# Spreading row sums and norm factors over the partitions by small DMAs through DRAM instead of TensorE transposes

## The chip, the cores and the metric

The kernel runs on one core of one Trainium2 chip. The metric is the device time of one execution in microseconds (us). An interval worked out from such times is given where two kernels are compared.

## The reference

Two layers (DEPTH = 2) of an encoder with 512 tokens and 1024 channels. One projection of the layer's input feeds everything: a latent attention (branch A), a differential attention (branch B), their SiLU gates, and the merge gates. Then the two branches are merged, projected, and normalized.

```python
for l in range(DEPTH):
    h = x @ w_in[l]
    c_q, c_kv, k_r, gate_a, q_d, k_d, v_d, gate_b, gates = _split_cols(h)
    q_a = (_rms_norm(c_q, g_q[l]) @ w_q_up[l])           # 8 heads, rotary on 32 of 96
    kv = (_rms_norm(c_kv, g_kv[l]) @ w_kv_up[l])          # 8 heads, keys 64 and values 64
    o_a = _dense_attention(q_a, k_a, v_a, mla_scale)      # softmax over 512 keys
    y_a = (o_a * jax.nn.silu(gate_a)) @ w_branch_a[l]
    o_b = _differential_attention(q_b, k_b, v_b, lam, diff_scale)   # 4 heads, 2 softmax maps each
    o_b = _rms_norm(o_b, g_diff[l], eps=1e-5) * (1.0 - lam_init)
    y_b = (o_b * jax.nn.silu(gate_b)) @ w_branch_b[l]
    g = jax.nn.sigmoid(gates + b_merge[l])
    out = (g[..., :D_MODEL] * y_a + g[..., D_MODEL:] * y_b) @ w_out[l]
    x = _layer_norm(DEEPNORM_ALPHA * x + out, ln_gamma[l], ln_beta[l])
```

## The kernel before

Activations stand feature-major: 128 features on the partitions, all 512 tokens along the free dimension. Every fp32 operand is split into a leading part and an exact rest, and a product is three matmuls: `mm3` (L122 to L125). ScalarE (ACT) makes the leading part, VectorE (DVE) the rest: for weights these are L109 and L112 in `slot`, for other tiles L159 and L160 in `split`.

A projection of 128 columns of `w_in` (`proj`) is 24 matmuls of 128x512 into one of three PSUM banks called `acc`. Scores go to two banks `sc`, transposes to two banks `tr` (in traces `pstr`), and attention outputs to one bank `pv`.

**Latent attention (the MLA stage).** For each of 8 heads, `mla_scores` makes four tiles of scores (128 queries by 512 keys), and `soft` takes the row maximum on DVE (L169) and the exponential on ACT (L171), whose accumulator leaves the row sum: one number per query, queries on the partitions. `mla_values` transposes the exponentials chunk by chunk on TensorE (`keyT`, L178), splits them (ACT L180, DVE L181), and multiplies by the values into `pv` (L365, L366). Two heads make one output chunk `o` of 128 features by 512 tokens. Its row sums stand with the tokens on the partitions, but have to multiply along the free dimension. So after the odd head the kernel takes reciprocals (L375), writes each 64 times side by side (`rx`, L377, DVE), transposes the result by four TensorE transposes with the identity into a `tr` bank (L381), multiplies the gate chunk by it (L383), and then the output by the gate (L384).

**Differential attention.** For each of 4 heads, `diff_scores` and `diff_values` do the same with two maps. The RMS norm factor of a token (four columns of 128) is computed by DVE (L481, L482) and by a power on GpSimd (POOL, L484). `bcast` spreads it over the partitions with four transposes of a column that is read 128 times (L140). L487 multiplies the gate by it, L488 the output by the gate, and `split` makes the operand of the second branch projection.

**Order.** Each engine works through its own list in order. A scheduling layer fixes these lists when the kernel is built, from the order in which the code emits the operations, and it lets operations that it expects to be ready go ahead of others. The code emits the work in the order of `weave` and of the tables `fill` and `dfill`: `fill[h]` names the projections emitted behind MLA head h ("a2" is the gate chunk 2, "q0" and "k0" are the queries and keys of differential head 0). Temporary tiles of 128x512 have the tag `tmp` with three buffers; gate chunks have the tag `g` with two. All DMAs are issued by SyncE (SP): the weights come as 512 KB tiles (L103). GpSimd issues none.

Of the kernel before, what the change touches and what calls it, by code (L numbers as in the profile page):

```python
# [11 lines left out]
F32 = mybir.dt.float32  # L12
F32R = mybir.dt.float32r
AF = mybir.ActivationFunctionType
ALU = mybir.AluOpType
# [4 lines left out]
SEQ = 512  # L20
P = 128
# [10 lines left out]
# columns of w_in  # L32
# [3 lines left out]
# Weight slots of one layer, in order of use: each is [128, 1024].  # L36
# [9 lines left out]
# columns of the parameter table  # L46
# [4 lines left out]
def hybrid_trunk(ctx: ExitStack, tc: tile.TileContext, x, xT, wlat, wts, prm, dlam, gb, tab, rtab, out):  # L51
# [29 lines left out]
    # ---- constants  # L81
# [5 lines left out]
    # the clock of TensorE rises while the first loads are on their way  # L87
# [12 lines left out]
    # ---- weight slots: H is the leading part of w, L the exact rest  # L100
# [14 lines left out]
    # x, feature-major  # L115
# [11 lines left out]
    def proj(l, name):  # L127
        """128 columns of w_in, feature-major: [128 features, 512 tokens]."""
        hi, lo = slot(l, name)
        acc = pt_("acc")  # L130
        for k in range(KC):
            mm3(acc, hi[:, k * P:(k + 1) * P], lo[:, k * P:(k + 1) * P],
                xH[:, k, :], xL[:, k, :], k == 0, k == KC - 1)
        return acc

    def bcast(col):
        """columns [128 tokens, 4] -> [128, 512] with the token's value in every row."""
        b = pt_("tr")
        for t in range(NT):
            nc.tensor.transpose(b[:, t * P:(t + 1) * P], col[:, t:t + 1].broadcast_to([P, P]), ident)  # L140
        return b

    def silu2(acc):
        """2*silu of a gate chunk."""
        th = t2("tmp")
        nc.scalar.activation(th, acc, AF.Tanh, scale=0.5)
        g = t2("g")
        nc.vector.scalar_tensor_tensor(g, th, 1.0, acc, ALU.add, ALU.mult)
        return g
# [16 lines left out]
    def soft(S, sums):  # L166
        """exp(S - max) with its row sums."""
# [6 lines left out]
    def keyT(pts, c):  # L174
        """chunk c of the keys of p, transposed: [128 keys, 512 queries], split."""
# [8 lines left out]
    def layer(l, last):  # L184
# [3 lines left out]
        # ---- latents and the shared rotary key, token-major, with the RMS norms  # L188
# [65 lines left out]
        # ---- lambda  # L254
# [15 lines left out]
        # ---- key tiles of the even and the odd heads: 64 rows without, 2 x 32 rows with rotary  # L270
# [71 lines left out]
        def mla_scores(h, q):  # L342
# [4 lines left out]
            sums = opair[-1][1].rearrange("p (t e) -> p t e", e=2)  # L347
            pts = []
            for t in range(NT):
# [4 lines left out]
                yield pts  # L354

        def mla_values(h, pts):
# [16 lines left out]
            if e == 1:  # L373
                r = small(8)
                nc.vector.reciprocal(r, sums)  # L375
                rx = t2("tmp")
                nc.vector.tensor_scalar(rx.rearrange("p (a b) -> p a b", a=8),  # L377
                                        r.unsqueeze(2).broadcast_to([P, 8, 64]), 0.5, None, ALU.mult)
                b = pt_("tr")
                for t in range(NT):  # L380
                    nc.tensor.transpose(b[:, t * P:(t + 1) * P], rx[:, t * P:(t + 1) * P], ident)  # L381
                g = gate_acc.pop(c)
                nc.vector.tensor_tensor(g, g, b, ALU.mult)  # L383
                nc.vector.tensor_tensor(o, o, g, ALU.mult)  # L384
                yA.append(split(o, "y"))
            yield

        # ---- differential attention
# [33 lines left out]
        def diff_v(c):  # L422
            """the values of heads 2c and 2c+1: [128 tokens, 2 x 128] for each token tile"""
# [68 lines left out]
        # ---- branch projections under their merge gates  # L492
# [28 lines left out]
        # ---- emission  # L521
        def weave(*gens):
            """One step of each in turn; what the first yields."""
# [33 lines left out]
        fill = {0: ["q0"], 1: ["k0"], 2: [], 3: ["q1"], 4: ["k1", "a2"], 5: [], 6: ["a3"], 7: []}  # L557
# [45 lines left out]
        # ---- out projection, residual, layer norm  # L603
# [79 lines left out]
# ---- host side: layout only  # L683
# [98 lines left out]
```

## Time and profile before

| | |
|---|---|
| median of 3 runs | 864.25 us (863.44 to 864.85) |
| profiled execution, first to last instruction | 862.9 us |
| TensorE (PE) matmuls busy | 848.3 us, 98% |
| VectorE busy | 588.8 us, 68% |
| ScalarE busy | 429.6 us, 50% |
| GpSimd busy | 21.8 us, 3% |
| mean DMA rate | 88 GB/s |

The one profiled execution's own time is known as this span; it lies 1.35 us under the median of the runs. "Busy" for PE counts from a matmul's start to its modelled end, and matmuls overlap, so the distance from start to start is the better measure of what one costs. The stages of layer 0 are, by the first and last instructions of their lines, about 45 to 160 us (MLA), 190 to 345 us (differential attention and branch projections woven with it), and after that the merge gates and the output projection; layer 1 repeats them from about 470 us.

### The profile page before, as it was taken

The page shows a single profiled execution, that of the slowest core. Times are in us where ns is not written, and L with a number is a line of the kernel's source. Part 1 is how long each engine was busy: PE and PEld are TensorE (multiplying, and loading weights), DVE is VectorE, ACT ScalarE, POOL GpSimd, SP SyncE. Part 2 cuts the span into 40 slices and gives each one's busy share as a digit, 9 for nine tenths or more (in the row PEclk, how much of TensorE's full clock was granted, in tenths as well). Part 3 has the DMA queues.
Part 4 walks back from the last instruction along what each step waited for, and adds up shares of the span by engine and source line. Part 5 has one row for each costly group of instructions (what it writes and reads, how often), then busy time and mean ns, then how long its engine had stood idle before and what let it go on. Part 6 is the DMA issues. An engine that isn't in the chain of part 4 may idle for free.

```text
span 862.9 us, 11026 instructions
## 1 busy us (share of the span) xinstructions
PE 848.3 (98%) x4121; PEld 693.9 (80%) x4121; DVE 588.8 (68%) x1066; ACT 429.6 (50%) x843; POOL 21.8 (3%) x30
## 2 busy tenths in 40 slices
PE   9899999999999999999999999999999999999996
PEld 7678777878888878888897778788788888788885
DVE  6689998686646745455857899876667466545457
ACT  5767776463534633332236776755546354433310
POOL 0100000000000000000110000000000000000001
PEclk9999999999999999999999999999999999999998
DMA  8310111213222352233514010112222234422322
GB/s 299 116 43 31 38 56 55 74 32 99 90 74 74 122 177 78 95 97 117 182 41 143 13 36 26 49 49 74 74 74 74 79 92 123 151 97 95 98 74 97
DMA packets 27701, 75.70 MB, mean 88 GB/s; under 512 B 3200, under 2 KB 7808, under 8 KB 27648
## 3 DMA queue, kind: packets, MB, share of 16 engines
q1 hardware_dynamic: 27648, 75.01, 27.0%
q8 instruction: 32, 0.52, 0.3%
q14 instruction: 21, 0.17, 0.1%
HBM read 70.80 MB, written 4.19 MB: 87 GB/s over the span
## 4 chain that ended last, share of the span: by engine, by line
PE 89%; ACT 5%; DVE 3%; DMA 1%; issue 1%; POOL 0%; SPq 0%; DVEq 0%; ACTq 0%
PE psacc L124 22%; PE psacc L123 22%; PE psacc L125 22%; PE pstr L178 4%; PE pspv L365 2%; PE pspv L123 2%; PE pssc L123 2%; PE pspv L366 2%; PE pssc L124 2%; PE pssc L125 2%; PE pspv L124 1%; PE pspv L125 1%; ACT wh L109 1%; PE pssc L444 1%; DMA wr<-in_wts_dram 1%; PE pssc L449 1%
## 5 line engine op out<-in xcount | busy, mean ns | idle before, releaser
L112 DVE TENSOR_TENSOR wl<-wr,wh 128x512 fp32r<-128x512 f32 x192 | 126.9, 686 | 152.3 <-ACT wh L109 152.0
L123 PE MATMUL psacc<-xH,wh 128*128 128x512 f32 x512 | 203.5, 398 | 0.0
L125 PE MATMUL psacc<-xH,wl 128*128 128x512 f32 x512 | 203.4, 397 | 0.0
L124 PE MATMUL psacc<-xL,wh 128*128 128x512 f32 x512 | 203.2, 397 | 0.0
L109 ACT CAST wh<-wr 128x1024 fp32r<-128x1024 f32 x96 | 100.6, 1048 | 180.6 <-PE psacc L124 95.6
L123 PEld LDWEIGHTS psacc<-xH,wh 128*128 128x128 f32 x512 | 96.2, 188 | 21.9
L124 PEld LDWEIGHTS psacc<-xL,wh 128*128 128x128 f32 x512 | 96.2, 188 | 21.8
L125 PEld LDWEIGHTS psacc<-xH,wl 128*128 128x128 f32 x512 | 96.3, 188 | 21.3
L171 ACT ACTIVATE p<-pssc,sm 128x512 f32<-128x512 f32 x128 | 88.2, 690 | 25.1 <-DVE sm L169 24.4
L169 DVE TENSOR_REDUCE sm<-pssc 128x1 f32<-128x512 f32 x128 | 86.7, 683 | 4.5 <-PE pssc L125 1.8
L181 DVE TENSOR_TENSOR pt<-pstr,pt 128x512 fp32r<-128x512 f32 x96 | 64.9, 685 | 8.5 <-ACT pt L180 7.9
L180 ACT CAST pt<-pstr 128x512 fp32r<-128x512 f32 x96 | 55.6, 586 | 27.8 <-PE pstr L178 25.7
L178 PE MATMUL pstr<-ident,p 128*128 128x128 f32 x384 | 57.3, 272 | 0.0
L178 PEld LDWEIGHTS pstr<-ident,p 128*128 128x128 f32 x384 | 47.4, 141 | 12.0 <-ACT p L171 0.5
L123 PE MATMUL psacc<-wh,xH 128*128 128x256 f32 (+1 forms) x164 | 49.1, 299 | 0.1
L124 PE MATMUL psacc<-wl,xH 128*128 128x256 f32 (+1 forms) x164 | 48.7, 297 | 0.2 <-DVE wl L202 0.2
L125 PE MATMUL psacc<-wh,xL 128*128 128x256 f32 (+1 forms) x164 | 48.3, 295 | 0.0
L123 PEld LDWEIGHTS psacc<-wh,xH 128*128 128x128 f32 x164 | 30.9, 188 | 1.5 <-ACT xH L119 0.6
L124 PEld LDWEIGHTS psacc<-wl,xH 128*128 128x128 f32 x164 | 30.9, 188 | 0.8 <-DVE wl L202 0.4
L125 PEld LDWEIGHTS psacc<-wh,xL 128*128 128x128 f32 x164 | 30.8, 188 | 0.2
L365 PE MATMUL pspv<-pt,vs 128*128 128x512 f32 x64 | 29.1, 455 | 0.3
L123 PE MATMUL pssc<-kv,qm 128*128 128x512 f32 x64 | 26.7, 422 | 0.4 <-ACT kv L322 0.3
(233 smaller groups left out, 1502.0 us busy)
## 6 DMA issues: line engine op xcount, KB each, us to landing
wr<-in_wts_dram SPq DMA_DIRECT2D x106, 512.0 KB, 3.5
p<-in_xT_dram SPq DMA_DIRECT2D x8, 256.0 KB, 5.0
qr<-in_wts_dram SPq DMA_DIRECT2D x16, 128.0 KB, 2.2
p<-in_gb_dram SPq DMA_DIRECT2D x8, 256.0 KB, 3.0
y<-in_x_dram SPq DMA_DIRECT2D x8, 256.0 KB, 5.2
x_scratch<-y SPq DMA_DIRECT2D x8, 256.0 KB, 2.1
y<-x_scratch SPq DMA_DIRECT2D x8, 256.0 KB, 4.7
out_dram<-y SPq DMA_DIRECT2D x8, 256.0 KB, 2.0
```

Source lines behind the costliest of these rows:

```text
L109: nc.scalar.copy(hi, raw)
L112: nc.vector.tensor_tensor(lo[:, c], raw[:, c], fr(hi[:, c]), ALU.subtract)
L123: nc.tensor.matmul(o, lhsT=lh, rhs=rh, start=start, stop=False)
L124: nc.tensor.matmul(o, lhsT=lh, rhs=rl, start=False, stop=False)
L125: nc.tensor.matmul(o, lhsT=ll, rhs=rh, start=False, stop=stop)
L169: nc.vector.tensor_reduce(m, S, axis=AX.X, op=ALU.max, negate=True)
L171: nc.scalar.activation(p, S, AF.Exp, bias=m, scale=1.0, accum_out=sums)
L178: nc.tensor.transpose(b[:, t * P:(t + 1) * P], pts[t][:, c * P:(c + 1) * P], ident)
L180: nc.scalar.copy(h, b)
L181: nc.vector.tensor_tensor(lo, b, fr(h), ALU.subtract)
L365: nc.tensor.matmul(pv, lhsT=v, rhs=ph, start=kc == 0, stop=False)
L366: nc.tensor.matmul(pv, lhsT=v, rhs=pl, start=False, stop=kc == NT - 1)
```

## The change

The helper `bcast` no longer uses TensorE. It writes the columns (128 tokens by 4, or by 8 where n = 2) to a small DRAM tile with the tokens side by side, by one GpSimd DMA whose elements of 4 bytes are placed one by one, and reads each row of 512 numbers back into all 128 partitions of a `tmp` tile by one GpSimd DMA (n = 1), or into 64 partitions each by two (n = 2). In the MLA stage the reciprocal, the factor 0.5, the broadcast and the multiplication of the gate move from the end of the odd head's `mla_values` to the end of its `mla_scores`, and the tile of 128x512 copies (`rx`) is gone. The row sums of the pair of heads are stored with the head as the outer index. The gate chunk has to exist earlier for this: "a2" moves from `fill[4]` to `fill[2]`, "a3" from `fill[6]` to `fill[4]`, and "k1" from `fill[4]` to `fill[5]`. (The changed file also drops comments; line numbers of the two files differ by a few.)

```diff
-    def bcast(col):
-        """columns [128 tokens, 4] -> [128, 512] with the token's value in every row."""
-        b = pt_("tr")
-        for t in range(NT):
-            nc.tensor.transpose(b[:, t * P:(t + 1) * P], col[:, t:t + 1].broadcast_to([P, P]), ident)
+    def bcast(col, n=1):
+        rows = dram.tile([n * NT, P], F32, tag=f"rows{n}", name=nm("rows"), bufs=2)
+        nc.gpsimd.dma_start(rows.rearrange("c p -> p c"), col, allow_slow_non_contiguous=True)
+        b = t2("tmp")
+        w = P // n
+        for e in range(n):
+            row = rows[e * NT:(e + 1) * NT].rearrange("(o t) p -> o (t p)", o=1)
+            nc.gpsimd.dma_start(b[e * w:(e + 1) * w, :], row.broadcast_to([w, SEQ]))
         return b
...
-            sums = opair[-1][1].rearrange("p (t e) -> p t e", e=2)
+            sums = opair[-1][1].rearrange("p (e t) -> p t e", e=2)
...
+            if e == 1:
+                r = small(8)
+                nc.vector.reciprocal(r, opair[-1][1])
+                nc.vector.tensor_scalar(r, r, 0.5, None, ALU.mult)
+                g = gate_acc[h // 2]
+                nc.vector.tensor_tensor(g, g, bcast(r, 2), ALU.mult)
...
             if e == 1:
-                r = small(8)
-                nc.vector.reciprocal(r, sums)
-                rx = t2("tmp")
-                nc.vector.tensor_scalar(rx.rearrange("p (a b) -> p a b", a=8),
-                                        r.unsqueeze(2).broadcast_to([P, 8, 64]), 0.5, None, ALU.mult)
-                b = pt_("tr")
-                for t in range(NT):
-                    nc.tensor.transpose(b[:, t * P:(t + 1) * P], rx[:, t * P:(t + 1) * P], ident)
                 g = gate_acc.pop(c)
-                nc.vector.tensor_tensor(g, g, b, ALU.mult)
                 nc.vector.tensor_tensor(o, o, g, ALU.mult)
...
-        fill = {0: ["q0"], 1: ["k0"], 2: [], 3: ["q1"], 4: ["k1", "a2"], 5: [], 6: ["a3"], 7: []}
+        fill = {0: ["q0"], 1: ["k0"], 2: ["a2"], 3: ["q1"], 4: ["a3"], 5: ["k1"], 6: [], 7: []}
```

How the lists move, at three places. First DVE at the end of the MLA stage of layer 0 (fourth output chunk), before: the reciprocal, the copies, and the multiplication that reads PSUM.

```order
L375 RECIPROCAL sm_1603<-sm_1343 128x8
L112 TENSOR_TENSOR wl_1664<-wr_1661,wh_1663 128x512
L372 TENSOR_TENSOR op_1342<-pspv_1447,tmp_1516 64x512
L148 SCALAR_TENSOR_TENSOR g_1553<-tmp_1551,psacc_1526 128x512
L181 TENSOR_TENSOR pt_1562<-pstr_1556,pt_1561 128x512
L181 TENSOR_TENSOR pt_1571<-pstr_1565,pt_1570 128x512
L112 TENSOR_TENSOR wl_1664<-wr_1661,wh_1663 128x512
L181 TENSOR_TENSOR pt_1582<-pstr_1576,pt_1581 128x512
L181 TENSOR_TENSOR pt_1593<-pstr_1587,pt_1592 128x512
L377 TENSOR_SCALAR tmp_1605<-sm_1603 128x512
L372 TENSOR_TENSOR op_1342<-pspv_1555,tmp_1600 64x512
L383 TENSOR_TENSOR g_1553<-g_1553,pstr_1607 128x512
```

The same place of the changed kernel. L363 is now a small operation, and the multiplication of the gate (L365) reads the tile that the DMAs fill.

```order
L362 RECIPROCAL sm_1549<-sm_1336 128x8
L363 TENSOR_SCALAR sm_1549<-sm_1549 128x8
L112 TENSOR_TENSOR wl_1990<-wr_1987,wh_1989 128x512
L186 TENSOR_TENSOR pt_1568<-pstr_1562,pt_1567 128x512
L186 TENSOR_TENSOR pt_1577<-pstr_1571,pt_1576 128x512
L112 TENSOR_TENSOR wl_1990<-wr_1987,wh_1989 128x512
L383 TENSOR_TENSOR op_1335<-pspv_1480,tmp_1558 64x512
L186 TENSOR_TENSOR pt_1588<-pstr_1582,pt_1587 128x512
L186 TENSOR_TENSOR pt_1599<-pstr_1593,pt_1598 128x512
L365 TENSOR_TENSOR g_1307<-g_1307,tmp_1554 128x512
L383 TENSOR_TENSOR op_1335<-pspv_1561,tmp_1606 64x512
L386 TENSOR_TENSOR op_1335<-op_1335,g_1307 128x512
```

Seven DVE operations of 128x512 now stand between the small operation whose result is written to DRAM and the multiplication that waits for its way back. At the other chunks it is seven (first), ten (second) and eight (third), and the same in layer 1.

Second, DVE at the last head of the differential attention of layer 0 in the changed kernel. `wl_3318` and `wl_3352` are weights of the next merge gates, `lat_3233` is the operand of the branch projection.

```order
L483 SCALAR_TENSOR_TENSOR sm_3188<-s_442_1773 128x4
L484 SCALAR_TENSOR_TENSOR sm_3188<-sm_3178,sm_3188 128x4
L112 TENSOR_TENSOR wl_3318<-wr_3315,wh_3317 128x512 x2
L489 SCALAR_TENSOR_TENSOR g_3011<-tmp_3229,gs_324,g_3011 128x512
L490 TENSOR_TENSOR op_3175<-op_3175,g_3011 128x512
L112 TENSOR_TENSOR wl_3352<-wr_3349,wh_3351 128x512
L165 TENSOR_TENSOR lat_3233<-op_3175,lat_3233 128x512
```

Two weight operations have moved ahead of the multiplication by the norm factor (before, L487 followed L482 at once). For the first two heads of a layer about thirty DVE operations stand between, for the third seven.

Third, GpSimd, which had only the powers here. L140 is the write of the columns, L145 the reads back.

```order
L140 DMA rows_1552<-sm_1549 128x8x1
L145 DMA tmp_1554<-rows_1552 64x512 x2
L486 TENSOR_TENSOR sm_1985<-sm_1982,mhalf 128x4
L140 DMA rows_2426<-sm_1985 128x4x1
L145 DMA tmp_2428<-rows_2426 128x512
L486 TENSOR_TENSOR sm_2472<-sm_2469,mhalf 128x4
L140 DMA rows_2929<-sm_2472 128x4x1
L145 DMA tmp_2931<-rows_2929 128x512
```

GpSimd's list now alternates powers and DMAs; in the MLA stage it holds only these DMAs, three for each chunk.

## The prediction

> **What bounds the kernel now.** I read the shares of the engines and the chain of waits on the page first, then the busy time by stage.
>
> ```profile
> PE 848.3 (98%) x4121; PEld 693.9 (80%) x4121; DVE 588.8 (68%) x1066; ACT 429.6 (50%) x843; POOL 21.8 (3%) x30
> PE 89%; ACT 5%; DVE 3%; DMA 1%; issue 1%; POOL 0%; SPq 0%; DVEq 0%; ACTq 0%
> ...
> core 0: us, PE busy (x) PEld busy (x) DVE busy (x) ACT busy (x) POOL busy (x), PEclk, DMA share, GB/s
> 45.00:160.00 115.00, 114.62 (x595) 92.83 (x594) 99.21 (x170) 78.32 (x158) 0.00 (x0) 1.00 0.14 46
> 190.00:345.00 155.00, 154.94 (x750) 127.15 (x750) 91.61 (x165) 69.12 (x132) 3.56 (x4) 1.00 0.32 100
> 470.00:587.00 117.00, 116.60 (x607) 94.90 (x606) 99.88 (x170) 78.69 (x158) 0.00 (x0) 1.00 0.14 42
> ```
>
> TensorE sets the end nearly everywhere: 89% of the chain. The stages differ in what stands next to it. In the MLA stage (45 to 160, 470 to 587) DVE is busy for 99.2 of 115 us, 86%, so a DVE that waits has little time to catch up. In the differential stage (190 to 345) it is 91.6 of 155 us, 59%. The granted clock is 1.00 in all of them.
>
> **What the change removes.** Sixteen groups of four transposes (8 of L381, 8 of L140).
>
> ```profile
> L381 PE MATMUL pstr<-ident,tmp x32: 270/272/273, 76.6 to 576.5; 128*128 128x128 f32 x32
> L140 PE MATMUL pstr<-ident,sm x32: 270/272/276, 234.4 to 750.3; 128*128 128x128 f32 x32
> L377 DVE TENSOR_SCALAR tmp<-sm x8: 417/418/419, 75.9 to 574.9; 128x512 f32<-128x512 f32 x8
> ...
> 76.40 0.40 PE L125 MATMUL psacc<-xH,wl 128*128 128x512 f32 x1
> 76.64 0.60 PE L381 MATMUL pstr<-ident,tmp 128*128 128x128 f32 x4
> 76.99 0.48 PE L123 MATMUL psacc<-xH,wh 128*128 128x512 f32 x1
> 77.31 0.40 PE L124 MATMUL psacc<-xL,wh 128*128 128x512 f32 x1
> 77.55 0.40 PE L125 MATMUL psacc<-xH,wl 128*128 128x512 f32 x1
> ```
>
> The 272 ns of one transpose overlap, so I take starts. A matmul follows the one before it after 77.55 - 77.31 = 0.24 us. From the group's start (76.64) to the second matmul behind it (77.31) are 0.67 us, in which one matmul has its 0.24. A group costs 0.67 - 0.24 = 0.43 us, and 16 of them 6.9 us: this is all that TensorE can give back. The eight of the differential stage, 3.5 us, I count in full, because PE has no idle time there (154.94 of 155). Of the eight in the MLA stage, some fill moments in which PE's next matmul would have waited anyway for DVE or ACT (0.4 of 115 us shows as idle, more is hidden in the overlapping ends); between 0 and 3.5 us come back, and I take the middle, 1.7. DVE loses eight copies of 0.42 us (L377); DVE is not what ends the chain, and I count nothing for them beside that middle. Gain: 3.5 + 1.7 = 5.2 us.
>
> **What it adds: a round trip L in place of a group.** The write of the columns, GpSimd's wait for it, the read back, and DVE's multiplication behind it. No GpSimd DMA is in this trace, so L is bounded by SP's DMAs.
>
> ```profile
> x_scratch<-y SPq DMA_DIRECT2D x8, 256.0 KB, 2.1
> out_dram<-y SPq DMA_DIRECT2D x8, 256.0 KB, 2.0
> qr<-in_wts_dram SPq DMA_DIRECT2D x16, 128.0 KB, 2.2
> p<-in_gb_dram SPq DMA_DIRECT2D x8, 256.0 KB, 3.0
> prms<-in_prm_dram SPq DMA_DIRECT2D x1, 20.0 KB, 4.4
> q1 hardware_dynamic: 27648, 75.01, 27.0%
> ...
> 76.93 0.33 SPq L103 DMA_DIRECT2D wr<-in_wts_dram  x1
> ```
>
> Write: at least 2.0 us, as a plain store to DRAM. But it has 128 x 8 = 1024 single elements, 64 on each of 16 DMA engines. The 27,648 packets of q1 took 27.0% of 16 x 862.9 us, 0.135 us each; if an element cost as much as such a packet of 2.7 KB, it would be 64 x 0.135 = 8.6 us more, 10.7 together. An element is 4 bytes, and the nearest row of short pieces is prms: 160 bytes per partition, landing after 4.4 us behind the first loads of the kernel. I take 3.6, between that row and the undisturbed store. Read: 2.2 us as qr, whose 128 KB are those of each read of the MLA form (64 partitions of 2 KB); the second read of the MLA form is issued behind the first, 0.33 us later if GpSimd issues like SP, and about 1.0 if it needs as long as for a power (the POOL row below). I take 1.0, from the nearest row of that engine. With 0.3 us for the two hand-overs, L = 3.6 + 2.2 + 1.0 + 0.3 = 7.1 us, between 4.5 (2.0 + 2.2 + 0.3) and 14.2 (10.7 + 3.5).
>
> The Trainium skill, page "DMA: Bandwidth & Descriptors", section "Anatomy of one DMA — SWDGE (gpsimd) path", fits such DMAs as about 2.0 us plus the bytes at 436 GB/s. By it L would be an estimated 5.6 us (2.0 + 2.3 + 1.0 + 0.3), and nothing would be exposed. No run here shows it yet.
>
> **What covers L in the MLA stage.** Behind the small operation L363, DVE does 7, 10, 8 and 7 operations before the multiplication: 8 on average.
>
> ```profile
> 74.09 0.68 DVE L112 TENSOR_TENSOR wl<-wr,wh 128x512 fp32r<-128x512 f32 x1
> 74.69 0.68 DVE L181 TENSOR_TENSOR pt<-pstr,pt 128x512 fp32r<-128x512 f32 x1
> 75.29 0.68 DVE L169 TENSOR_REDUCE sm<-pssc 128x1 f32<-128x512 f32 x1
> ...
> 127.04 0.69 DVE L181 TENSOR_TENSOR pt<-pstr,pt 128x512 fp32r<-128x512 f32 x1
> 128.39 0.69 DVE L181 TENSOR_TENSOR pt<-pstr,pt 128x512 fp32r<-128x512 f32 x1
> 128.50 0.39 PE L366 MATMUL pspv<-pt,vs 128*128 128x512 f32 x1
> 129.64 0.40 PE L366 MATMUL pspv<-pt,vs 128*128 128x512 f32 x1
> ```
>
> They start 0.60 us apart where nothing is waited for (74.09, 74.69, 75.29), and about 0.72 where one needs another; 8 at 0.62 are 5.0 us of work, and at DVE's 86% 5.8 us pass. Some of the eight wait for PE (L383 for the end of a head's values, L328 for new keys), so I take 6.2; by the count of operations alone the four chunks lie between 5.0 and 7.2. What does a late multiplication delay? Everything behind it on DVE: the rest of the transposed exponentials (L186), the row maxima (L174), the key rests (L328), and PE's value and score matmuls behind these. PE has little in hand: L181 ends at 127.04 + 0.69 = 127.73 and its reader L366 starts at 128.50, 0.8 us later; the next pair is 129.08 and 129.64, 0.6. So each chunk absorbs 0.7 us, and beyond 6.2 + 0.7 = 6.9 us every microsecond of L is lost at 8 places. At L = 7.1 this is 0.2 x 8 = 1.6 us.
>
> **The differential heads.** For heads 0 to 2 of a layer a projection and up to thirty DVE operations lie between: more than 10 us, no cost. The last head is tight:
>
> ```profile
> 322.09 1.01 POOL L484 TENSOR_TENSOR sm<-sm,mhalf 128x4 f32<-128x4 f32 x1 [25.68 <-DVE sm L482]
> 324.30 0.75 DVE L487 SCALAR_TENSOR_TENSOR g<-pstr,gs,g 128x512 f32<-128x512 f32 x1 [2.28 <-PE pstr L140]
> 326.94 0.69 DVE L160 TENSOR_TENSOR lat<-op,lat 128x512 fp32r<-128x512 f32 x1
> 329.70 0.40 PE L123 MATMUL psacc<-lat,wh 128*128 128x512 f32 x1
> 331.77 0.39 PE L123 MATMUL psacc<-lat,wh 128*128 128x512 f32 x1
> ```
>
> The power ends at 323.10. From L487 (324.30) to the finished operand (327.63) are 3.3 us, and the branch projection reads this fourth chunk only with its tenth matmul, at 331.77. A trip of 331.77 - 3.3 - 323.1 = 5.4 us is hidden. With half the elements, I take 2.8 for the write (the 1.5 over the store, halved), 2.6 for the single read of 256 KB (between the 2.2 of qr and the 3.0 of gb, whose loads queue behind each other) and 0.3: 5.7 us, 0.3 too long, twice: 0.6 us. At the bounds (4.5, and 2.0 + 4.3 + 3.0 + 0.3 = 9.6) it is 0 and 8.4 us. The weights queued behind (`wl_3352`) are those of the fourth merge gate, which PE reaches after the two branch products and the third gate, some 11 us later.
>
> **The moved gate chunks.** The same 24 matmuls, the same DVE and ACT operations, at other places of a stage in which PE is full at either place. Their weight loads on SP move along. I count zero, between -1 and +1 us. The DMAs of GpSimd add 16 x 256 KB, on engines that are busy 14% in the MLA stage.
>
> **Sum.** -5.2 + 1.6 + 0.6 + 0 = -3.0 us: span 862.9 - 3.0 = 859.9, and for the median of the runs, which lies 1.35 us above the span, 864.25 - 3.0 = 861.3 us (861.25 rounded).
>
> **Rivals.** (1) *Hidden fully*: L at most 6.9, and the last heads' trip at most 5.4. Then -5.2 us, 859.1; if all of the MLA groups come back, -6.9, 857.4. For it: plain DMAs here take 2.0 to 2.2 us each. Against: elements of 4 bytes, and the engine that issues. The fit of the Trainium skill named above leads here.
>
> (2) *Slower: the trip is longer than its cover.* The eight multiplications in the MLA stage stop DVE, in order, and PE runs dry behind it. The price is 8 us for each us of L over 6.9; it pays back the 5.2 - 0.6 = 4.6 us at L = 6.9 + 4.6 / 8 = 7.48, and is 0.2% slower from L = 7.69. At L = 9 (a write of 5.5) it is 2.1 x 8 - 4.6 = +12.2 us, 876.5; at the upper bound of 14.2, +53.8, 918. For it: 1024 single elements, two reads issued one after the other, and 86% DVE. Against: only 14% DMA load in that stage. The same page of the Trainium skill, "Rules for kernel authors", says that a last dimension that is not contiguous becomes one descriptor per element, which it advises against; no row here prices one.
>
> (3) *No change*: L between 7.26 and 7.69, or a trip that is hidden while the MLA groups and part of the others had been filling waits; within 1.7 us of 864.25.
>
> (4) *The change doesn't do what it says*: excluded for the transposes, since their rows are gone from PE's list.
>
> **Chances.** The three runs before differ by 0.16%, so 0.2%, 1.7 us, is about what can be told from no change. L up to 7.26: 0.47, of which 0.25 for the forecast (the trip exposed by a little) and 0.22 for rival 1. Rival 3, even: 0.14. Rival 2, slower: 0.39, spread over a long stretch of L. The predicted time is the forecast's, 861.3 us; faster cases have the range 858.0 to 862.5. The whole range reaches to L = 9.1 at the upper end, 877.0; 0.13 is left out above and 0.05 below 858.0.
>
> **What would show it.** Right: PE has 64 transposes fewer; DVE's idle time before L365 with a DMA as releaser is under 1 us each, before L489 of the last head some 3 us; the MLA stage keeps its 115 us. Wrong: idle time of 2 us or more before each of the eight L365, with PE idle behind it and an MLA stage longer by four times the excess; or a read that is issued late because GpSimd waits for a `tmp` buffer. The landing times of the two kinds of DMA give L directly.

## The result: 11% slower

The changed kernel takes 962.4 us (median of 4 runs, 960.35 to 970.07) against 864.5 us for the kernel before. The medians are 97.9 us apart; the ratio of the runs is 1.1146, 95% interval 1.1122 to 1.117. The prediction was 861.3 us with a range of 858.0 to 877.0. The execution that was profiled is the longest of the four, span 968.3 us, 105.4 more than the profiled one of the kernel before.

The page of the changed kernel: busy time of each engine, the granted clock over the span, and the chain of work that ended last.

```profile
PE 874.7 (90%) x4057; PEld 707.7 (73%) x4057; DVE 587.9 (61%) x1066; ACT 427.6 (44%) x843; POOL 51.2 (5%) x70
...
PEclk9997987999999987999999988979799999979999
...
PE 64%; DMA 14%; DVE 8%; issue 6%; ACT 6%; POOL 1%; SPq 0%; DVEq 0%; POOLq 0%; ACTq 0%
```

The 64 transposes are gone (4057 instead of 4121 matmuls), yet TensorE's share fell from 98% to 90%, and in the chain DMA rose from 1% to 14%. PE's busy time *rose*, from 848.3 to 874.7 us, though it has less to do: the clock row, which was 9 throughout, has eights and sevens in it. The mean granted clock is 0.945 instead of 0.997.

The waits (engine, tile and line that waited, what for, us in total, times, longest):

```profile
POOL tmp L145 <- DMA rows<-sm: 77.7, 8, 11.9
DVE g L365 <- DMA tmp<-rows: 67.0, 8, 9.6
PE pspv L377 <- DVE pt L186: 45.5, 6, 8.8
DVE g L489 <- DMA tmp<-rows: 26.8, 4, 12.2
```

DVE stands still for 67.0 us in all before the eight gate products of MLA (L365), 8.4 us each where the prediction allowed under 1, and PE stands behind it (L377). The last differential heads add most of 26.8 us (L489). One MLA place in order of time (start, duration, engine, line):

```profile
62.00 1.07 POOL L140 DMA_DIRECT2D rows<-sm  x1 [34.93 <-DVE sm L363]
72.91 1.06 POOL L145 DMA_DIRECT2D tmp<-rows  x2 [9.83 <-DMA rows<-sm]
73.15 0.40 PE L123 MATMUL psacc<-xH,wh 128*128 128x512 f32 x1
76.25 0.69 DVE L365 TENSOR_TENSOR g<-g,tmp 128x512 f32<-128x512 f32 x1 [7.90 <-DMA tmp<-rows]
81.07 0.79 PE L377 MATMUL pspv<-pt,vs 128*128 128x512 f32 x1 [7.53 <-DVE pt L186]
```

GpSimd issues the write at 62.0, may read back only at 72.9, and the product starts at 76.25: a round trip of 14.25 us instead of the 7.1 predicted. PE runs dry at 73.5, and its next matmul, at 81.07, takes 0.79 us instead of 0.40. The DMA table (KB each, median us from issue to landing) says which half is late:

```profile
tmp<-rows POOLq DMA_DIRECT2D x16, 128.0 KB, 3.1
tmp<-rows POOLq DMA_DIRECT2D x8, 256.0 KB, 4.0
rows<-sm POOLq DMA_DIRECT2D x8, 4.0 KB, 10.0
rows<-sm POOLq DMA_DIRECT2D x8, 2.0 KB, 9.4
```

The reads take 3.1 and 4.0 us where the prediction counted 2.2 and 2.6; the writes of 4 and 2 KB take 10.0 and 9.4 us where it counted 3.6 and 2.8. So most of the excess is in the write. PE's busy time and granted clock around the same place, by stretches of the span:

```profile
core 0: us, PE busy (x), PEclk, DMA share, GB/s
62.00:73.00 11.00, 10.82 (x50) 1.00 0.04 0
73.00:81.00 8.00, 0.55 (x3) 0.74 0.09 33
81.00:87.00 6.00, 5.93 (x18) 0.50 0.00 1
87.00:106.00 19.00, 18.78 (x91) 1.00 0.23 70
```

The trace's clock records have 0.50 from 76.8, when PE has stood idle for 3.3 us, to 87.1. There are 12 such stretches, beside one at the very end that the kernel before has too. At 0.50 a matmul follows the one before after 0.43 instead of 0.23 us, so about half of the time that PE is busy there is lost. Over the whole trace PE's idle times of 0.5 us or more (from 45 us on) come to 80.1 us, against 2.5 before, and PE is busy for 60.0 us at 0.50, of which half is 30.0.

### The profile page after: what moved, and what is told of

It is laid out like the page before. It is cut to its first block, busy times and chain, and to the rows that moved or that the text cites. A ratio compares the mean times of both kernels' runs of the same rounds, so it can differ in the third digit from the quotient of the medians.

```text
span 968.3 us, 10961 instructions
## 1 busy us (share of the span) xinstructions
PE 874.7 (90%) x4057; PEld 707.7 (73%) x4057; DVE 587.9 (61%) x1066; ACT 427.6 (44%) x843; POOL 51.2 (5%) x70
## 4 chain that ended last, share of the span: by engine, by line
PE 64%; DMA 14%; DVE 8%; issue 6%; ACT 6%; POOL 1%; SPq 0%; DVEq 0%; POOLq 0%; ACTq 0%
PE psacc L124 16%; PE psacc L123 16%; PE psacc L125 16%; DMA rows<-sm 7%; DMA tmp<-rows 4%; PE pstr L183 3%; DMA wr<-in_wts_dram 2%; PE pspv L377 1%; PE pspv L123 1%; PE pspv L124 1%; PE pspv L125 1%; PE pspv L376 1%; PE pssc L123 1%; ACT wh L109 1%; PE pssc L124 1%
## 5 line engine op out<-in xcount | busy, mean ns | idle before, releaser
L112 DVE TENSOR_TENSOR wl<-wr,wh 128x512 fp32r<-128x512 f32 x192 | 127.2, 687 | 163.7 <-ACT wh L109 163.4
L123 PE MATMUL psacc<-xH,wh 128*128 128x512 f32 x512 | 205.8, 402 | 5.1 <-DVE g L153 4.9
L124 PE MATMUL psacc<-xL,wh 128*128 128x512 f32 x512 | 206.7, 404 | 0.0
L125 PE MATMUL psacc<-xH,wl 128*128 128x512 f32 x512 | 206.5, 403 | 0.0
L125 PEld LDWEIGHTS psacc<-xH,wl 128*128 128x128 f32 x512 | 98.3, 192 | 22.3
L124 PEld LDWEIGHTS psacc<-xL,wh 128*128 128x128 f32 x512 | 98.3, 192 | 22.2
L377 PE MATMUL pspv<-pt,vs 128*128 128x512 f32 x64 | 29.1, 455 | 45.5 <-DVE pt L186 45.5
L183 PE MATMUL pstr<-ident,p 128*128 128x128 f32 x384 | 61.5, 290 | 0.0
L183 PEld LDWEIGHTS pstr<-ident,p 128*128 128x128 f32 x384 | 51.1, 151 | 11.6 <-issue 2.3
L377 PEld LDWEIGHTS pspv<-pt,vs 128*128 128x128 f32 x64 | 13.4, 210 | 51.7 <-DVE pt L186 50.1
L365 DVE TENSOR_TENSOR g<-g,tmp 128x512 f32<-128x512 f32 x8 | 5.5, 692 | 67.0 <-DMA tmp<-rows 67.0
L123 PE MATMUL psacc<-lat,wh 128*128 128x512 f32 x64 | 27.0, 422 | 17.7 <-ACT lat L164 17.7
```

Of the source, the lines that this page charges most:

```text
L112: nc.vector.tensor_tensor(lo[:, c], raw[:, c], fr(hi[:, c]), ALU.subtract)
L123: nc.tensor.matmul(o, lhsT=lh, rhs=rh, start=start, stop=False)
L124: nc.tensor.matmul(o, lhsT=lh, rhs=rl, start=False, stop=False)
L125: nc.tensor.matmul(o, lhsT=ll, rhs=rh, start=False, stop=stop)
L183: nc.tensor.transpose(b[:, t * P:(t + 1) * P], pts[t][:, c * P:(c + 1) * P], ident)
L377: nc.tensor.matmul(pv, lhsT=v, rhs=pl, start=False, stop=kc == NT - 1)
```

## The experiments

Five groups: what the spread itself is worth, where the 98 us lie, why the write is late, whether the low clock needs a DMA, and a mended change. The table gives medians of the runs in us, with the kernel before of the same series beside it, and then the us of each stage in the profiled execution. A stage is the distance between marks in the trace: the first value matmul of MLA, the first value matmul of the differential heads, and the first matmul of the second branch projection. The third column runs on from there to the next layer's first mark, in layer 1 to the end of the last matmul.

| Kernel | time (before beside it) | MLA, layer 0 / 1 | differential | branch projection and on |
|---|---|---|---|---|
| before | 864.5 | 123.4 / 123.5 | 151.2 / 151.0 | 151.8 / 99.5 |
| the change | 962.4 (864.5) | 161.3 / 161.6 | 155.4 / 153.4 | 163.3 / 110.7 |
| no spread | 859.25 (864.86) | 122.6 / 122.5 | 149.3 / 149.3 | 152.2 / 99.5 |
| order only | 869.14 (864.86) | 125.7 / 125.6 | 151.2 / 151.2 | 151.4 / 99.5 |
| chunks only | 865.88 (864.86) | 124.0 / 123.9 | 151.2 / 151.1 | 151.8 / 99.5 |
| MLA by DMA | 938.04 (864.48) | 159.9 / 159.4 | 151.1 / 151.0 | 152.5 / 99.5 |
| differential by DMA | 894.96 (864.48) | 123.5 / 123.4 | 154.5 / 155.3 | 163.4 / 111.5 |
| runs of 16 bytes | 876.08 (864.86) | 126.3 / 127.2 | 150.1 / 150.1 | 156.0 / 103.6 |
| mended | 863.76 (864.86) | 123.2 / 123.1 | 150.8 / 150.8 | 151.7 / 99.5 |

**What the spread is worth.** The change with nothing spread at all:

```diff
     def bcast(col, n=1):
-        (write to DRAM, reads back)
+        return tabs[:, 1, :]
```

> The change without any spreading: the multiplications read a table that is there from the start instead of the spread factors, so neither transposes nor DMAs are left at the 16 places (the factors are left out of the result). This is the gain of the change with a round trip that costs nothing. If the prediction's gain term is right, it gains 5.2 us on the kernel before, with 3.5 and 6.9 us as ends: 857.4 to 861.0, ratio 0.992 to 0.996. If the transposes had been hidden by other work, it stays at 863.5 to 865. The granted clock stays at 1.0 and no wait ahead of the multiplications remains.

Measured: 859.25 us (859.19 to 859.88), ratio 0.9938 (0.9921 to 0.9955): -5.6 us.

```profile
PE 843.0 (98%) x4057; PEld 687.3 (80%) x4057; DVE 587.4 (69%) x1066; ACT 429.9 (50%) x843; POOL 21.8 (3%) x30
...
PEclk9999999999999999999999999999999999999999
```

PE's busy time is 5.3 us less than before, and the clock is 9 throughout. The gain term of the prediction, 5.2 us, holds: the differential groups give 1.7 to 1.9 us per layer, the MLA stage 0.8 to 1.0. No round trip in this order can be expected to gain more.

The new order with the transposes kept, and, after it, only the two gate chunks moved:

```diff
+            if e == 1:                      # at the end of mla_scores
+                ... the four transposes, and g multiplied by them
-                ... the same at the end of mla_values
-        fill = {..., 2: [], 3: ["q1"], 4: ["k1", "a2"], 5: [], 6: ["a3"], 7: []}
+        fill = {..., 2: ["a2"], 3: ["q1"], 4: ["a3"], 5: ["k1"], 6: [], 7: []}
```

> The new order alone (the gate multiplied by the factors at the end of the second head's scores, the two gate chunks moved), with the transposes of the kernel before in place of the DMAs. The prediction put this at 0 plus or minus 1 us: 863.5 to 865.5. If part of the 98 us came from the new order rather than from the DMAs, it is 868 or more.

Measured: 869.14 us (868.68 to 869.56), ratio 1.005 (1.0035 to 1.0065): +4.3 us, all of it in the MLA stage (+2.2 in each layer).

> The kernel before with only the two gate chunks moved. The new order with transposes took 4.6 us more than before (869.14 us), where the prediction had 0 plus or minus 1. If the moved chunks carry that, 868 to 870; if it is the place of the transposes (the queue of TensorE then has them at the end of the scores, where it waits for the row sums), 863.5 to 865.5.

Measured: 865.88 us, ratio 1.0011 (1.0002 to 1.002): +1.0 us. So the moved chunks cost about 1 us, the edge of what was predicted, and the rest of the 4.3 comes with the transposes at the new place. The change has no transposes there, and the run without any spreading, which has the same order, is quicker than the kernel before in that stage.

**Where the 98 us lie.** One half of the change each:

```diff
     def bcast(col, n=1):
+        if n == 1:      # MLA by DMA; in the other kernel, only the differential heads by DMA
+            b = pt_("tr") ... four transposes
+            return b
```

> The change, but the eight spreads of the differential heads are done by transposes as before; only the MLA spreads go through DRAM. By the marks in the trace of the change (the gate products of MLA end 45.5 and 42.5 us later per layer, of which 12 and 11 are caught up by the first differential head) the MLA part is worth 65 us: 925 to 940. If the two parts hold each other up, the two halves add up to much less than 98 us.

> The kernel before, with only the eight spreads of the differential heads through DRAM. By the marks in the trace of the change the last head of each layer is 19 us later against the third, and heads 0 to 2 together 3 us; some 10 us of the last are caught up behind it: 885 to 900. The prediction's price for this part was 0.6 us and its gain 3.5.

Measured: 938.04 us (ratio 1.085, 1.0818 to 1.0881), +73.6; and 894.96 us (ratio 1.0352, 1.0314 to 1.0389), +30.5. The first is at the upper end of what was expected, the second inside. Together they cost 104.0, six more than the whole change, and the table puts them where the whole has them. The six do not show that the halves overlap: they come from the choice of executions. The profiled executions of the halves are 73.3 and 31.6 us longer than that of the kernel before, together 104.9, and the whole change's, its longest, is 105.4 longer. The change's runs differ by 9.7 us, and the longer ones have the lower mean clock (970.07, 963.95, 960.86 and 960.35 us with 0.945, 0.954, 0.959 and 0.961). In the differential half, the last head of layer 0, in order of time:

```profile
327.92 0.79 POOL L138 DMA_DIRECT2D rows<-sm  x1 [0.29 <-POOL sm L487]
...
341.89 0.75 DVE L490 SCALAR_TENSOR_TENSOR g<-tmp,gs,g 128x512 f32<-128x512 f32 x1 [12.09 <-DMA tmp<-rows]
...
344.08 0.80 PE L123 MATMUL psacc<-lat,wh 128*128 128x512 f32 x1 [8.78 <-ACT lat L162]
```

14.0 us from the write's issue to the product, 12.09 of them with DVE idle, and PE idle for 8.78.

**Why the write is late.** The kernel before, with an unread write of the same columns beside each transpose group, in eight forms (shortened; each is used twice in one execution, once in each kind of attention):

```diff
+        if v == 0: nc.gpsimd.dma_start(D([n, P]).rearrange("c p -> p c"), col)      # as in the change
+        elif v == 1: nc.gpsimd.dma_start(D([P, n]), col)                           # a run per partition
+        elif v == 2: nc.sync.dma_start(D([n, P]).rearrange("c p -> p c"), col)
+        elif v == 3: nc.gpsimd.dma_start(D([P, n, 128])[:, :, 0], col)             # 512 bytes apart
+        ...
```

> The kernel before with one extra small write of the row sums or norm factors at each of its 16 spreads; nothing reads what is written, so the result and the chain are the kernel before's, and the time should stay within 2 us of 864 (only the write that SyncE issues can hold up its queue). Eight kinds, each used twice, so that the time from issue to landing of each can be set beside the 10.0 us (1024 elements) and 9.4 us (512 elements) of the change: (v0) as in the change: GpSimd, 4-byte elements scattered into DRAM; (v1) GpSimd, one contiguous run of 32 or 16 bytes per partition in DRAM; (v2) as v0, but issued by SyncE; (v3) GpSimd, each 4-byte element alone in its own 512 bytes of DRAM; (v4) GpSimd, 4-byte elements scattered into the chip's SBUF; (v5) as v0 with one column, 128 elements; (v6) as v1, each run in its own 512 bytes; (v7) as v0 from 32 partitions, a quarter of the elements. Theory 1, a write of single 4-byte elements into DRAM is acknowledged late: v0, v2, v3, v5 and v7 at 8 to 12 us, v1, v4 and v6 at 2 to 4. Theory 2, every small write that GpSimd issues is late: all at 8 to 12 but v2 at 2 to 4. Theory 3, the price goes with the number of elements: v0, v2, v3, v4 at 9 to 12, v7 at 4 to 5, v1, v5 and v6 at 2 to 4. Theory 4, elements of one stretch of DRAM that come from several DMA engines hold each other up: v0, v2, v5 and v7 at 8 to 12, v1 between, v3, v4 and v6 at 2 to 4.

Each source line with its two issues (duration of the issue in ns, first and last start), and the time from issue to landing; in order v0, v1, v2, v3:

```profile
L151 POOL DMA_DIRECT2D pr<-sm x2: 815/942/1069, 73.0 to 616.8; - x2
DMA to landing us min/median/max: 10.2/10.4/10.6
...
L153 POOL DMA_DIRECT2D pr<-sm x2: 567/582/596, 97.7 to 668.4; - x2
DMA to landing us min/median/max: 1.7/2.1/2.4
...
L155 SPq DMA_DIRECT2D pr<-sm x2: 378/380/381, 130.2 to 722.4; - x2
DMA to landing us min/median/max: 8.5/8.7/9.0
...
L157 POOL DMA_DIRECT2D pr<-sm x2: 733/794/855, 141.7 to 749.3; - x2
DMA to landing us min/median/max: 2.2/2.7/3.3
```

The others, medians of two: v4, into SBUF, 2.5 us; v5, 128 elements, 8.6; v6, runs in 512 bytes of their own, 2.6; v7, a quarter of the elements, 7.2. The time of the kernel was 865.3 us (one run). Every theory but the fourth falls. Not the engine that issues: GpSimd lands runs in 2.1 us, SyncE needs 8.7 for the scattered form. Not the count: 128 elements side by side take 8.6 us, 1024 that lie 512 bytes apart 3.3 (the slower use of v3; the other has 512). Not DRAM and not 4 bytes alone, by the same v3. The fourth theory is not right in all of its numbers either: it expected v7 at 8 us or more, and v1 between the late and the quick forms. What is left is that single elements, each from another partition, lie next to each other in DRAM. (v4 says nothing on this: its elements lie 32 bytes apart.) The second set varies the spacing:

```diff
+        nc.gpsimd.dma_start(D([P, k])[:, 0:1], col[:, 0:1])       # k = 2, 4, 8, 16, 32, 64 elements apart
+        nc.gpsimd.dma_start(D([8, 16]).rearrange("b a -> a b"), col[:, 0:1])    # v6: neighbours from partitions 8 apart
+        nc.gpsimd.dma_start(D([P, 2]), col[:, 0:2])               # v7: runs of 8 bytes
```

> The kernel before with an unread write beside each spread, as in the first set of landings, which left two readings of theory 4. All are issued by GpSimd; (v0) to (v5) write one column of 128 elements with 8, 16, 32, 64, 128 and 256 bytes from one partition's element to the next one's (4 bytes took 8.6 us there, 512 bytes 2.7 us); (v6) writes them 4 bytes apart, but with the order changed so that neighbours in DRAM come from partitions 8 apart; (v7) writes runs of 8 bytes, one per partition, side by side. Reading 4a, the elements that fall into one block of DRAM are taken one after the other: the landing above 2.2 us falls in proportion as the spacing grows, about half at each doubling (8 bytes 5 to 6 us, 16 bytes 3.5 to 4.5, 32 bytes 2.5 to 3.5, from 64 bytes on 2 to 3), v6 as 4 bytes (8 to 9), v7 5 to 6. Reading 4b, only neighbours that the same DMA engine writes hold each other up: v6 falls to 2 to 4 us. Theory 1, any single 4-byte element is late, was refuted by v3 of the first set. The time stays within 2 us of 864.5.

The time was 864.76 us (one run). The same view; 8 bytes, 16 bytes, and v6:

```profile
L151 POOL DMA_DIRECT2D pr<-sm x2: 595/658/722, 72.6 to 617.1; - x2
DMA to landing us min/median/max: 3.7/3.8/4.0
...
L153 POOL DMA_DIRECT2D pr<-sm x2: 546/570/595, 97.2 to 668.7; - x2
DMA to landing us min/median/max: 1.8/2.3/2.8
...
L163 POOL DMA_DIRECT2D pr<-sm x2: 554/573/592, 296.7 to 556.3; - x2
DMA to landing us min/median/max: 6.2/6.9/7.6
```

| bytes from element to element | 4 | 8 | 16 | 32 | 64 | 128 | 256 | 512 |
|---|---|---|---|---|---|---|---|---|
| median landing of two, us (4 and 512: first set; 512 with 1024 and 512 elements, the others with 128) | 8.6 | 3.8 | 2.3 | 2.5 | 2.1 | 2.0 | 2.3 | 2.7 |

Runs of 8 bytes land in 3.3 us, where 4a had 5 to 6. Reading 4a holds in direction, but the fall is steeper than it said: from 16 bytes on nothing is left. Reading 4b, with 2 to 4 us for v6, misses the measured 6.9 us; that partitions 8 apart go through different DMA engines is assumed in it, as the trace does not tell which engine carries an element. The packets are not late: in the change's own trace those of a write have ended 2.3 us (MLA) and 1.8 us (differential, medians) after the issue, and the completion follows 6.3 to 9.3 us later. That elements side by side in one small block of DRAM hold each other up fits the direction of all this, not the steep fall; what does so, and the size of the block, the trace does not show.

The change with runs of 16 bytes instead of scattered elements, and a multiplication that reads them with a stride:

```diff
-        nc.gpsimd.dma_start(rows.rearrange("c p -> p c"), col, allow_slow_non_contiguous=True)
+        nc.gpsimd.dma_start(rows.rearrange("(e p) t -> p e t", e=n), col.rearrange("p (e t) -> p e t", e=n))
...
-            row = rows[e * NT:(e + 1) * NT].rearrange("(o t) p -> o (t p)", o=1)
+            row = rows[e * P:(e + 1) * P].rearrange("(o p) t -> o (p t)", o=1)
...
-        return b
+        return b.rearrange("w (p t) -> w t p", t=NT)
```

> The change with one thing altered: each partition's four factors lie side by side in DRAM, so that the first DMA writes runs of 16 bytes instead of single 4-byte elements; the reads back are of the same size, and the multiplication reads the spread tile with a stride. Theories 1 and 3 (the 4-byte elements are what is late): the write lands 2 to 4 us after its issue, the whole round trip takes 6.5 to 9 us instead of 14.2, DVE waits less than 3 us before each gate multiplication of MLA, the granted clock stays above 0.99, and the time is 858 to 880. Theory 2 (any small write by GpSimd): the landing stays at 9 to 12 us and the time at 955 to 970.

Measured: 876.08 us (874.25 to 877.99), ratio 1.013 (1.011 to 1.0151). Its DMA rows and its waits:

```profile
rows<-sm POOLq DMA_DIRECT2D x8, 4.0 KB, 2.5
rows<-sm POOLq DMA_DIRECT2D x8, 2.0 KB, 1.7
```

```profile
DVE g L366 <- DMA tmp<-rows: 10.6, 6, 4.1
DVE g L491 <- DMA tmp<-rows: 9.0, 2, 4.6
```

The landing fell from 10.0 to 2.5 and from 9.4 to 1.7 us, and 87 of the 98 us went with it. So in the change itself, too, it is the form of the write that is late, and not the engine that issues it. The 67.0 us before the MLA product became 10.6; one of the waits, 4.1 us, is longer than the 3 that were expected. What remains stands in two places of the table: the MLA stage (+2.9 and +3.7), and the last head (+4.2 and +4.1), whose trip of 6.3 and 6.5 us is still longer than the 5.4 that hide it.

The stride has a price of its own. The MLA product in the change, and here:

```profile
L365 DVE TENSOR_TENSOR g<-g,tmp x8: 691/692/693, 76.2 to 674.0; 128x512 f32<-128x512 f32 x8
...
L366 DVE TENSOR_TENSOR g<-g,tmp x8: 1060/1082/1109, 69.0 to 594.7; 128x512 f32<-128x512 f32 x8
```

It takes 1.08 instead of 0.69 us, and the product of the differential heads 1.13 instead of 0.75: 6.2 us more DVE work over the 16 places. How much of it reaches the end no run isolates.

**Whether the low clock needs a DMA.** No spread at all, and before each MLA product one DVE reduction that only takes time (the factors are left out here too, and the product has a constant in their place):

```diff
+                nc.vector.tensor_reduce(late, tabs[:, 1, :].unsqueeze(1).broadcast_to([P, k, 512]), axis=AX.XY, op=ALU.max)
+                nc.vector.scalar_tensor_tensor(g, g, late, bcast(r, 2), ALU.mult, ALU.mult)      # bcast returns tabs[:, 1, :]
-                nc.vector.tensor_tensor(g, g, bcast(r, 2), ALU.mult)
```

> No spreading at all (as in the run without transposes and DMAs, 859.25 us), but ahead of each gate multiplication of MLA one DVE reduction that only takes time, over 4, 8, 12 and 16 times 512 elements in layer 0 and 6, 10, 14 and 18 times 512 in layer 1, about 0.6 us for each 512. So DVE is late by 2.4 to 10.8 us at the eight places, and there is no DMA in it. Theory A, the granted clock of TensorE falls when TensorE has been idle for several us, whatever made it idle: TensorE stands idle behind the long reductions, the clock goes to 0.5 behind each idle time above some bound between 3 and 7 us and to nothing behind the short ones; the time is 859 plus the idle times plus about 2 us for each dip, 895 to 925. Theory B, the low clock of the change belongs to its DMAs: the clock stays at 1.0, and the time is 890 to 910.

Measured: 883.62 us (one run), below both forecasts: the longest reductions, at the last place of each layer (8.7 and 9.7 us), left PE idle for less than 1 us at a time. So the time does not decide between the theories, but the clock does. At the second place (k = 8), the reduction and PE's next matmul; then PE's busy time and granted clock around it:

```profile
93.81 4.41 DVE L361 TENSOR_REDUCE sm<-tabs 128x1 f32<-128x4096 f32 x1
...
99.82 0.73 PE L373 MATMUL pspv<-pt,vs 128*128 128x512 f32 x1 [3.56 <-DVE op L380]
```

```profile
core 0: us, PE busy (x), PEclk, DMA share, GB/s
75.00:95.00 20.00, 19.56 (x95) 1.00 0.19 61
95.00:99.00 4.00, 1.25 (x9) 1.00 0.00 0
99.00:103.00 4.00, 3.18 (x7) 0.61 0.00 0
103.00:125.00 22.00, 21.99 (x107) 0.99 0.11 31
```

PE was idle for 3.56 us, and the clock fell, with DMA at 0.00. Four idle times did this (3.56, 1.98, 3.99, 3.24 us); the low stretches are 3.41, 3.41, 6.83 and 3.41 us long. Theory B falls: idle time of TensorE is enough, here with a long DVE operation as its cause. Theory A's bound of 3 to 7 us falls too, as 1.98 us did it.

**A mended change.** Runs of 16 bytes, the MLA product moved into the value loop, and transposes for the last differential head:

```diff
+                if e == 1 and kc == LATE:      # in mla_values; LATE = 1, then 3
+                    gv = gate_acc[c].rearrange("p (t q) -> p t q", t=NT)
+                    nc.vector.tensor_tensor(gv, gv, facs.pop(c), ALU.mult)
...
+            b = spread(r) if h == 3 else bcast(r)      # spread: four transposes
```

> A mended change. Each factor quartet is written as one run of 16 bytes (landing about 2.5 us instead of 10.0); the gate product of MLA stands one step and a half later in the program, so that the round trip of about 7 us has more than the 6.9 us of cover that the prediction counted; the last differential head of each layer, whose cover is 5.4 us, is spread by transposes. From the run without any spreading (859.25 us) plus two groups of transposes (0.9 us): 859.5 to 861.5, ratio 0.994 to 0.997, with the granted clock at 1.0 and no wait for the spread tiles left. If the GpSimd transfers cost something beside their latency, 862 to 866.

> As the mended change, the gate product of MLA two steps later still. If one step left some of the round trip uncovered, this is faster than it by up to 2 us; if the spread tile, which holds one of three shared buffers for longer, gets in the way of others, slower by 1 us or more. Otherwise the same within 0.5 us.

> As the run before, but with the two gate chunks where the kernel before has them. If the moved chunks cost the 4.6 us of the new order, this is up to 4 us faster, 855 to 858; if not, the same within 1 us.

Measured: 863.76 us (ratio 0.9985, 0.9976 to 0.9994), 863.42 us (0.9982, 0.9973 to 0.999), and, with the chunks where they were, 867.49 us (1.003, 1.002 to 1.0039). So the mended kernels are 1.1 and 1.4 us below the kernel before: both intervals lie just under 1, and both differences under the 0.2% that the prediction took as the least that can be told. The first misses its forecast of 859.5 to 861.5 us. The later product makes no difference. The chunks back in place make it 4 us slower, which neither branch of the expectation had: in this form the moved chunks gain 4 us, where among the transposes they cost 1, and why stays open. A wait of the first:

```profile
DVE g L386 <- DMA tmp<-rows: 5.2, 2, 2.6
```

Little of the trip shows: DVE waits twice, 2.6 us, at the last pair of each layer. Yet it is 4.5 us above the run without spreading, of which the two groups of transposes kept in it explain 0.9 by the prediction's 0.43 for a group. The table has the loss in the MLA stage (0.6 per layer) and the differential heads (1.5 per layer). In the two MLA stages 8 pairs of matmul starts are 0.5 to 1.0 us apart, and none without spreading. The second branch of the expectation, that the GpSimd transfers cost something beside their latency, fits the time (862 to 866). But the strided products are a rival that no run separates from it: at 14 places they take 0.38 to 0.39 us longer, 5.4 us of DVE time in all. Which of the two it is stays open.

## Why the prediction was wrong

**The step that failed** is the write of the round trip: "I take 3.6, between that row and the undisturbed store." It measured 10.0 us (MLA) and, where the prediction took 2.8, 9.4 (differential). The row chosen as nearest is a read of 160 bytes per partition; no row of the profile before has single elements side by side in DRAM, and with runs of 16 bytes the same write lands in 2.5 us. The bound of 10.7 held for the median by luck (two of the writes took 11.2 and 12.1): it priced 64 elements per engine, and the runs show that the count is not what costs. With the write, L became 14.6 on average (13.45 to 16.07) instead of 7.1. This is rival 2, and at L = 14.2 it gave 918.

**The price beyond the cover was also too low: it had no term for the clock.** It said one us for each us of L beyond the cover, at 8 places: 8 x (14.6 - 6.9) = 62 us. The MLA stages are 77.9 us longer than without any spreading. PE's idle times of 0.5 us or more in them come to 28.0 + 27.3 = 55.3 us, somewhat under the 62. The rest is the low clock: half of the time that PE is busy at 0.50 is 9.8 + 10.8 = 20.6 us, and with it 75.9 of the 77.9 are found. The prediction read the clock as 1.00 in every stage of the kernel before and put this term at nothing. The same holds for the last heads: PE's idle times there are 8.90 and 8.78 us, as the step would have it (14.0 - 5.4 = 8.6), and half of the busy time at 0.50 adds 2.3 and 2.1; the stretch behind is 11.2 us longer in both layers than without spreading.

**What held.**
- *Gain* 5.2: 5.6 measured without a round trip. Between 0 and 3.5, middle 1.7, for MLA gave 1.9 (0.84 + 1.02), net of the moved chunks; that the middle came so close is partly luck.
- *Cover in MLA* 6.2: the trip less DVE's wait is 6.35, 6.10, 6.55 and 5.83 us in layer 0, and 6.37, 6.12, 6.55 and 5.86 in layer 1, mean 6.2.
- *Cover of the last head* 5.4: 8.78 us of PE idle time at 14.27 us from the end of the power to the product, so 5.5 hidden. The price that it gave (0.6) followed from the wrong L.
- *Read, second issue and hand-overs* 3.5: 3.3 to 4.5 us from the read's issue to the product at the eight MLA places, mean 3.8. For the last heads it doesn't hold: the prediction had 2.9 there, and 4.3 and 4.0 were measured.
- *Moved chunks* 0, between -1 and +1: +1.0 among the transposes. In the mended change it doesn't hold: there they gain 4.
- *The read is late because GpSimd waits for `tmp`*, listed as a sign of failure: heads 0 and 1 do this, 26.6 to 26.8 us behind the write, and it costs nothing, as their product stands 38 to 40 us behind the write in the quick form as well.

**Heads 0 to 2 "no cost"** was too kind to head 2. With the slow write its product comes 16.5 to 18.7 us after the issue instead of 14.6 with the quick one, and the differential stage is 4.2 and 2.4 us longer than before, 6.1 and 4.1 longer than without spreading. Here the read is late as well: it lands after 7.9 and 6.4 us, where the median is 4.0. DVE's own wait is only 1.65 and 0.82 us, but PE stands idle for 2.78 and 2.37 us, and half of its busy time at 0.50 behind that is 3.3 and 1.7 us: 6.1 and 4.1 together.

**The two rules weighed in the prediction.** The Trainium skill, page "DMA: Bandwidth & Descriptors", section "Anatomy of one DMA — SWDGE (gpsimd) path", with its 2.0 us plus the bytes at 436 GB/s, agrees with the runs of 32 and 16 bytes (2.1 us) and not with the scattered form (10.0). By it the two kinds of read would take an estimated 2.3 and 2.6 us; they took 3.1 and 4.0. Its "Rules for kernel authors" advised against one descriptor per element. In this kernel that advice would have decided rightly, but the 1024 separate elements that landed in 3.3 us show that the count is not the reason.

## What to carry to other kernels

Before a small DMA replaces work of an engine, price its completion, not its bytes. Write one run per partition: single elements side by side in DRAM took 6 to 8 us longer here than elements 16 bytes apart or runs of 16 bytes. The reader's stride is much cheaper, but not free (0.39 us more for a product of 128x512 on DVE). An in-order engine that waits for the DMA stops everything behind it: DVE's 7.9 us left PE idle for 7.5. So the trip has to fit into what stands between the issue and the first use on that engine (6.2 us here, and 5.4 at the last head). And a long idle time of TensorE costs more than its length, as PE comes back at half clock. Even so, the best mended round trip was worth 1.4 us, where no spread at all was worth 5.6.

## What the hardware showed that was not expected

- A scattered write whose packets have ended 2.3 us after its issue was complete only at 10 us. From SyncE it is the same: the packets had ended after 1.6 us, and the write was complete at 8.5.
- Each idle time of PE of 6.5 us or more in the change was followed by a clock of 0.50, for 6.83 or 10.24 us; the shorter ones there (2.0 to 2.9 us, some of them in pairs) by 3.41 to 10.24. Even 1.5 us can do it, though not each time. In the kernel with runs of 16 bytes PE was idle for 1.67 us from 130.1, and no low stretch followed; at the last head of layer 0 it was idle for 1.51 us from 334.0 and 0.22 us later on, and one did. PE's busy time and clock around both:

```profile
core 0: us, PE busy (x), PEclk, DMA share, GB/s
128.50:131.91 3.41, 1.74 (x8) 1.00 0.00 0
131.91:135.32 3.41, 3.41 (x18) 1.00 0.02 5
333.30:336.72 3.42, 1.68 (x7) 1.00 0.00 0
336.72:340.13 3.41, 3.41 (x10) 0.50 0.52 156
```

The Trainium skill, page "TensorE: Matmul & The Clock Gate", section "Why this matters for your kernels", asks for no idle gap of TensorE above about 3 us. The stretches after 3.2 to 8.9 us agree; those after 1.5 to 2.9 us do not.

In these traces it goes by how much idle time falls into one fixed step of 3.41 us, not by the length of one gap. The low stretches of the change begin at 76.84, 117.80, 151.93 and 203.13 us, which are 12, 10 and 15 times 3.413 apart, and so on through each trace. The windows above are such steps. In the five traces with low stretches before the end, all 29 steps at full clock in which PE was idle for 1.87 us or more were followed by 0.50, none of those with 1.67 or less was, and of three between (1.74 to 1.81) one was. So about half a step is the bound here. The clock came back only behind a step in which PE was hardly idle (0.4 us at most), which is why a long idle time costs two or three steps.
